# A rank projection in two products instead of three, an earlier sixth product in Strassen rows, and finer task steps, in a two-layer backbone on one core

## The chip, the cores and the metric

The kernel runs on one core of a Trainium2 chip. The metric is the time of one launch on the device, in microseconds (us). Engines are called as in the profile: PE (TensorE: matrix products), DVE (VectorE), ACT (ScalarE), POOL (GpSimd) and SP (SyncE, which issues most DMAs).

## The reference, cut to what matters

One inference step of a two-layer diffusion backbone over 128 context and 512 latent tokens, model width 2048. Each layer is a modulated RMS norm, one wide in-projection, two mixers side by side, a SiLU gate, an output projection and a gated residual. Layer 0 mixes by windowed attention and by gated linear attention (GLA), layer 1 by neighbourhood attention and a gated MLP.

The part whose products the change rewrites is the low-rank gate of the GLA. The in-projection yields, besides q, k, v and the gates, 2 x 16 columns `rb`; they go through small weights to the gate of each channel:

```python
GLA_RANK = 16
EVEN_SPLITS = (H_A * HEAD_DIM, KV_A * HEAD_DIM, KV_A * HEAD_DIM,
               H_B * DK_B, H_B * DK_B, H_B * DV_B, 2 * GLA_RANK, MIX_W)
...
    r = rb.reshape(B, T, 2, GLA_RANK)
    logit = jnp.einsum('btdr,drk->btdk', r, wg) + bg
    g = (jax.nn.log_sigmoid(logit.astype(jnp.float32)) / GLA_NORMALIZER).reshape(B, T, 2, H_B, DK_B)
```

All is float32.

## The kernel before, in words

**Products.** Every float32 operand is split in two parts of a shorter format, a high part `h` (ACT writes it, a copy with rounding) and a low part `l` (POOL or DVE: the value less the high part). In the trace these are `acth`/`actl` for activations, `whi`/`wlo` for weights, `eh`/`el` and `fh`/`fl` for sums. A product is three matmuls into the same bank of accumulators: hi by h, hi by l, lo by h (`mm_k`, L862). The activations lie feature by feature: 16 columns k of 128 features by 640 tokens, and each matmul takes one k and one half of the tokens (320 columns, 322 where two columns of shift ride along).

**Weights.** `wpump` (from about L790) loads weight tiles ahead of their use, copies the high part with ACT and subtracts with POOL or DVE. For the rank projection `w_rb` (L2513, `add(d["w_rb"], 96, ...)`) the 32 columns are written three times, as three blocks of a stationary operand of 96 columns; rows 0 to 95 of the result then hold r three times, which `gla_rank` (L2010) splits into high and low for the next product with `wgs` (three blocks likewise, `gla_wg`, L2000).

**Layer-0 in-projection.** `chunk` and `units` (L887) run over chunks of 128 output columns, four k at a time for each half, and call `tick` on the way. There are three banks for these sums; a bank is emptied by DVE (`lin`: `arena<-bank,rstd`, then `bc<-bank`) once its last matmul is done. `tick(n)` (L543) lets waiting tasks make up to n steps: the steps of the GLA scan, the attention heads, the rewriting. What is left of DVE's time goes to the `low` task, the reductions of the adaLN weights (`ada`), which are a DVE instruction of 512 elements each. A model of the engines' times (`Pace`, L41) decides when a task may step; it runs while the program is built, so the order of each engine's instructions is fixed. `calm(lag)` (L575) lets a task go on only when the modelled queues of DVE and ACT are at most `lag` us ahead.

**Output projections and layer 1.** They use Strassen's scheme over pairs of output chunks, in rows: `steps` (L658) gives the order of the products of a pair (A11, A12, S1, S2, S4, S3, A22), `spair` (L1000) issues them, `strassen_jobs` (L671) the sums of weights that they need. The last pair of each of three rows (`ends`) reloads, behind its S3, the half columns of `acth`/`actl` that were folded to sums (`unfold`, L1258, DMAs `acth<-bh_dram`), which the next plain pair needs.

**Handover** (L1127). Between two layers the result, column by column, is scaled and split into `acth`/`actl` (`rewrite`, an order of k given by hand), and for the pairs of columns the half sums `eh`/`el` are formed (`fold`, with `split`, L1175). Three handovers are in the program: y0 (at about 800 us), x1 (about 1050) and y1. `rewrite` and `fold` share DVE and ACT, and both wait by `calm(3.0)`.

Of the kernel before, what the change touches and what calls it, by code (L numbers as in the profile page):

```python
# [245 lines left out]
class Trunk:  # L246
# [412 lines left out]
    def steps(self, c1, c2):  # L659

        names = lambda *x: [(c1, f) for f in x]
        if self.count[c1] == ALL:
            return names("A11", "A12", "S1", "S2", "S4", *(("S3", "A22") if c1 in self.ends else ("A22", "S3")))
        return [*names("A11"), (c1, PLAIN, 0), *names("A12", "S1", "S2", "S4"), (c2, PLAIN, 0), *names("S3", "A22")]
# [7 lines left out]
    def strassen_jobs(self, c1, c2, last, unit):  # L672
# [25 lines left out]
        add = lambda o, a, b, op: ("add", lambda: (piece(o), piece(a), piece(b)), op, 4 in (o, a, b))  # L698
# [9 lines left out]
        if ns == ALL:  # L708
            after = {("A12", 8): [add1], ("S1", 5): [add2], ("S2", 5): [add3], ("S4", 5): [add4]}
            assert all(t in [k + m for k, m in self.blocks_of(ns, f)] for f, t in after)  # L710
# [43 lines left out]
    def wpump(self, force=False):  # L754
# [63 lines left out]
        if m < M:  # L818
            raw = raw[:, :, None, :].to_broadcast([128, n, M // m, m])
            hi, lo = (x.rearrange("p a (b c) -> p a b c", c=m) for x in hl)  # L820
        nc.scalar.activation(hi, raw, AF.Copy)
# [40 lines left out]
    def mm_k(self, c, k, outs, first=0, last=KT - 1, r=0):  # L862
# [4 lines left out]
        todo = []  # L867
        for p, half in outs:
            cs = self.cols(half, shift)
            h, l = self.ah[:, k, cs], self.al[:, k, cs]  # L870
            todo += [(0, p, hi, h, k == first, False), (1, p, hi, l, False, False), (2, p, lo, h, False, k == last)]
# [11 lines left out]
    def units(self, c, k0, evac):  # L883

        p, done = [], self.ahead.pop(c, None)
        for k in range(k0, KT, 4):
            for half in range(2):  # L887
                if k == k0:
                    p.append(done if half and done is not None else self.pj())
                for j in range(k, k + 4):  # L890
                    if p[half] is not done:
                        self.mm_k(c, j, [(p[half], half)], k0)
                    if j % 2:
                        self.tick(2)
# [90 lines left out]
    def spair(self, c1, c2):  # L985
# [70 lines left out]
        end = self.steps(c1, c2)[-1]  # L1056
        for key in self.steps(c1, c2):
            f = key[1]
            if len(key) == 3 and key[0] == c1:
# [10 lines left out]
            elif f == "S1":  # L1070
                plus(full(xa), x)
                ev1(xa, None)
                self.drop(xa)
                v = take()
                self.need("T124")
                product(v, full, f, tt(0))
            elif f == "S2":
                product(t, full, f, tt(1))
                x = copy(half(t))
                plus(x, half(v))  # L1080
            elif f == "S4":
# [4 lines left out]
                self.drop(xb)  # L1086
            elif f == "S3":
                self.need("T3")
                product(t, half, f, J(x2))
                if c1 in self.ends:  # L1090
                    self.spawn(self.unfold(ns), first=True)
# [2037 lines left out]
```

## Time and profile before

| | |
|---|---|
| median of 3 runs | 2050.56 us (2047.29 to 2052.04) |
| the profiled execution's own time | 2051.18 us |
| its span in the trace | 2049.4 us |
| mean granted PE clock | 0.996 |
| PE instructions | 14255 |

The page gives shares of the span; the table of stretches cuts the span at given times and gives each engine's busy time there; the timeline gives single instructions in the form "start, duration, engine, line, operation, out<-in, shape", and in square brackets how long the engine stood idle before and which result ended that. L219 is the line of a helper through which all engine instructions go, L449 that of all matmuls, L454 of transpositions on PE, L492 of SP's DMAs. Durations of matmuls overlap: the pace is read from start to start.

### The profile page before, as it was taken

The numbers are of one execution on the slowest core, as the hardware profiler recorded it, in microseconds if no ns is written. First come the engines' busy times: TensorE is split into PE (matmuls) and PEld (weight loads), VectorE is DVE, ScalarE is ACT, GpSimd is POOL, SyncE is SP. The second block draws the span as 40 slices with busy tenths as digits, with TensorE's granted clock in tenths as the row PEclk, the third lists the DMA queues.
The fourth block names the chain that finished last, engine by engine and source line by source line (L and its number), as shares of the span: only waits on it lengthen the run. The fifth ranks groups of instructions, "written<-read, shape, count | busy, mean of one in ns | idle before, by whom it ended". The sixth has DMA issues, their size and how long they took to land.

```text
span 2049.4 us, 40331 instructions
## 1 busy us (share of the span) xinstructions
PE 2012.4 (98%) x14255; PEld 1976.9 (96%) x14255; DVE 1356.0 (66%) x3175; ACT 1098.7 (54%) x2430; POOL 1362.9 (67%) x1096
## 2 busy tenths in 40 slices
PE   8999999999999999999999999999999999999997
PEld 6899999999999999999989999999999999999997
DVE  4656677476557666898577787656665677568444
ACT  5445555445564766544465444565565654455443
POOL 5555465446556555798755777766766688878884
PEclk9999999999999999999999999999999999999999
DMA  9965433336456455577534434444344354265437
GB/s 376 400 208 163 143 112 102 121 119 185 156 184 215 148 179 179 174 242 230 186 107 138 134 126 132 133 132 130 120 147 126 120 174 154 91 216 194 144 98 277
DMA packets 234316, 344.13 MB, mean 168 GB/s; under 512 B 22049, under 2 KB 139649, under 8 KB 234113
## 3 DMA queue, kind: packets, MB, share of 16 engines
q1 hardware_dynamic: 232912, 340.38, 50.7%
q8 instruction: 112, 1.84, 0.4%
q10 hardware_dynamic: 1200, 1.17, 0.2%
q14 instruction: 92, 0.75, 0.1%
HBM read 304.99 MB, written 33.85 MB: 165 GB/s over the span
## 4 chain that ended last, share of the span: by engine, by line
PE 87%; DMA 6%; DVE 3%; ACT 2%; issue 1%; POOL 1%; SPq 0%; DVEq 0%; POOLq 0%; ACTq 0%
PE bank L449 84%; PE bank L454 2%; DMA more<-ada 1%; DMA Y<-ada 1%; DVE bank L219 1%; DVE arena L219 1%; DVE Y L219 1%; DMA arena<-yT_dram 1%; PE bank L1605 0%; DMA Y<-xT 0%; ACT acth L219 0%; DMA wraw<-w_even 0%; DMA wraw<-w_out 0%; DVE rs L219 0%; DMA rawx<-ada_g 0%
## 5 line engine op out<-in xcount | busy, mean ns | idle before, releaser
L449 PE MATMUL bank<-acth,whi 128*128 128x320 f32 (+3 forms) x3072 | 941.0, 318 | 6.8 <-DVE bc L219 2.8
L449 PE MATMUL bank<-actl,whi 128*128 128x320 f32 (+3 forms) x3072 | 917.0, 310 | 1.3 <-POOL actl L219 1.3
L449 PE MATMUL bank<-acth,wlo 128*128 128x320 f32 (+3 forms) x3072 | 915.6, 310 | 0.0
L219 POOL TENSOR_TENSOR wlo<-wraw,whi 128x512 fp32r<-128x512 f32 (+2 forms) x415 | 531.3, 1290 | 395.3 <-ACT whi L219 360.4
L449 PEld LDWEIGHTS bank<-acth,whi 128*128 128x128 f32 (+1 forms) x3072 | 569.1, 188 | 14.7 <-issue 4.1
L449 PEld LDWEIGHTS bank<-actl,whi 128*128 128x128 f32 (+1 forms) x3072 | 569.6, 188 | 3.5 <-POOL actl L219 1.5
L449 PEld LDWEIGHTS bank<-acth,wlo 128*128 128x128 f32 (+1 forms) x3072 | 568.6, 188 | 0.8 <-POOL wlo L219 0.6
L219 POOL TENSOR_TENSOR wlo<-rs,whi 128x384 fp32r<-128x384 f32 (+2 forms) x370 | 457.7, 1262 | 111.4 <-ACT whi L219 78.5
L219 ACT ACTIVATE whi<-wraw 128x512 fp32r<-128x512 f32 (+2 forms) x425 | 245.8, 586 | 164.1 <-PE bank L449 85.2
L219 ACT ACTIVATE whi<-rs 128x384 fp32r<-128x384 f32 (+2 forms) x370 | 191.9, 536 | 100.8 <-PE bank L449 45.7
L449 PE MATMUL bank<-eh,whi 128*128 128x322 f32 (+1 forms) x666 | 209.5, 314 | 0.0
L449 PE MATMUL bank<-el,whi 128*128 128x322 f32 (+1 forms) x666 | 206.4, 310 | 0.0
L449 PE MATMUL bank<-eh,wlo 128*128 128x322 f32 (+1 forms) x666 | 206.3, 310 | 0.0
L219 POOL TENSOR_TENSOR prod<-adas,mixrow 128x512 f32<-128x512 f32 x93 | 121.1, 1313 | 50.6 <-ACT prod L219 32.4
L219 DVE TENSOR_TENSOR bank<-bank,sums 128x320 f32<-128x320 f32 (+1 forms) x148 | 70.1, 495 | 95.8 <-ACT sums L219 47.9
L449 PEld LDWEIGHTS bank<-eh,whi 128*128 128x128 f32 x666 | 125.4, 188 | 0.0
L449 PEld LDWEIGHTS bank<-eh,wlo 128*128 128x128 f32 x666 | 125.4, 188 | 0.0
L449 PEld LDWEIGHTS bank<-el,whi 128*128 128x128 f32 x666 | 125.3, 188 | 0.0
L219 DVE CUSTOM_DVE_ANT_0 adas<-adas,bank,part 128x512 bf16<-128x512 f32 x146 | 108.6, 744 | 22.6 <-DMA adas<-ada 15.7
L219 POOL TENSOR_TENSOR wlo<-adas,whi 128x512 fp32r<-128x512 f32 x62 | 80.2, 1300 | 44.0 <-ACT whi L219 43.5
L219 ACT ACTIVATE sums<-bank 128x320 f32<-128x320 f32 (+1 forms) x111 | 48.2, 434 | 103.6 <-PE bank L449 97.4
L219 DVE CUSTOM_DVE_ANT_0 adas<-adas,bank 128x512 bf16<-128x512 f32 x107 | 73.2, 684 | 13.6 <-DMA adas<-ada 5.2
(287 smaller groups left out, 3057.6 us busy)
## 6 DMA issues: line engine op xcount, KB each, us to landing
wraw<-w_even SPq DMA_DIRECT2D x176, 256.0 KB, 3.3
rs<-w_odd SPq DMA_DIRECT2D x150, 256.0 KB, 3.3
adas<-ada SPq DMA_DIRECT2D x128, 256.0 KB, 3.8
adas<-ada_g SPq DMA_DIRECT2D x64, 256.0 KB, 3.8
rs<-w_out SPq DMA_DIRECT2D x60, 256.0 KB, 3.7
adas<-w_odd SPq DMA_DIRECT2D x50, 256.0 KB, 3.8
Y<-ada SPq DMA_DIRECT2D x24, 512.0 KB, 7.7
more<-ada SPq DMA_DIRECT2D x24, 512.0 KB, 7.8
```

The costliest lines, as they stand in the source:

```text
L219: return f(*args, **kw)
L449: self.nc.tensor.matmul(out, lhsT, rhs, start=start, stop=stop, **kw)
L454: self.nc.tensor.transpose(out, in_, self.ident[:k, :k])
```

## The change

Four edits.

1. The rank projection takes 128 columns, the 32 weight columns four times: blocks low, high, high, high. One product of 128 columns (all blocks by h) and one of 32 columns (a high block by l, into rows 0 to 31) take the place of three products of 96 columns, for each k and half: 64 matmuls instead of 96. The next product contracts 128 rows instead of 96.
2. In a row's last pair of 25 pairs' rows the order is A11, A12, S2, S1, S3, S4, A22 (before: A11, A12, S1, S2, S4, S3, A22); in the last pair of the row of output projection 0 S3 comes ahead of the second plain product. The last weight sum is made in two halves.
3. The half sums of a handover wait by `calm(1.5)` instead of 3.0 until the last column is rewritten.
4. In `units` tasks may make one step after an even k and two after an odd one, instead of two after an odd one.

The diff's core:

```diff
@@ steps
         if self.count[c1] == ALL:
-            return names("A11", "A12", "S1", "S2", "S4", *(("S3", "A22") if c1 in self.ends else ("A22", "S3")))
-        return [*names("A11"), (c1, PLAIN, 0), *names("A12", "S1", "S2", "S4"), (c2, PLAIN, 0), *names("S3", "A22")]
+            return names("A11", "A12", *(("S2", "S1", "S3", "S4", "A22") if c1 in self.ends else ("S1", "S2", "S4", "A22", "S3")))
+        last = [*names("S3"), (c2, PLAIN, 0)] if c1 in self.ends else [(c2, PLAIN, 0), *names("S3")]
+        return [*names("A11"), (c1, PLAIN, 0), *names("A12", "S1", "S2", "S4"), *last, *names("A22")]
@@ strassen_jobs
             after = {("A12", 8): [add1], ("S1", 5): [add2], ("S2", 5): [add3], ("S4", 5): [add4]}
+            if c1 in self.ends:
+                after = {("A11", 8): [add1], ("A12", 4): [add2], ("S2", 5): [add3], ("S1", 5): [add(4, 3, 2, ALU.subtract, (0, 4))], ("S1", 8): [add(4, 3, 2, ALU.subtract, (4, 8))]}
@@ wpump
         if m < M:
-            raw = raw[:, :, None, :].to_broadcast([128, n, M // m, m])
-            hi, lo = (x.rearrange("p a (b c) -> p a b c", c=m) for x in hl)
-        nc.scalar.activation(hi, raw, AF.Copy)
+            hi, lo = hi.rearrange("p a (b c) -> p a b c", c=m), hi[:, :, 0:m]
+            nc.scalar.activation(hi, raw[:, :, None, :].to_broadcast([128, n, M // m, m]), AF.Copy)
+            hi, hl = lo, [hl[0], hl[0]]
+        else:
+            nc.scalar.activation(hi, raw, AF.Copy)
@@ mm_k
+            if m < M:
+                n = h.shape[1]
+                self.mm(p[:M, :n], hi, h, start=k == first, stop=k == last, skip_group_check=True)
+                self.mm(p[:m, :n], hi[:, m : 2 * m], l, start=False, stop=k == last, skip_group_check=True)
+                continue
@@ units
-                    if j % 2:
-                        self.tick(2)
+                    self.tick(1 + j % 2)
@@ handover, split
-            yield from self.calm(self.calms[1])
+            yield from self.calm(self.calms[1] if f"{ready}:{order[-1]}" in self.flags else 1.5)
@@ gla_dir, gla_rank, in-projection, weights
-            self.mm(ps[:, :HT], L["wgs"][0:96, 128 * dr : 128 * dr + 128], L["r"][0:96, c])
+            self.mm(ps[:, :HT], L["wgs"][:, 128 * dr : 128 * dr + 128], L["r"][:, c])
...
-        nc.scalar.activation(r[0:96, :], x[0:96, :], AF.Copy)
-        nc.vector.tensor_tensor(r[64:96, :], x[64:96, :], r[64:96, :].bitcast(F32), ALU.subtract)
+        nc.scalar.activation(r, x, AF.Copy)
+        nc.vector.tensor_tensor(r[96:128, :], x[96:128, :], r[96:128, :].bitcast(F32), ALU.subtract)
...
-        add(d["w_rb"], 96, True, None, lazy("vt", rows=96, then=lambda x: self.spawn(self.gla_rank(x))))
+        add(d["w_rb"], 128, True, None, lazy("vt", then=lambda x: self.spawn(self.gla_rank(x))))
```

Edits 3 and 4 change the order of the engines' instructions through the model. Two places show how.

On DVE, in the layer-0 in-projection at 338 to 346 us of the trace before: `Y` and the first operand `arena` are the GLA's scan (the two `SCALAR_TENSOR_TENSOR` rows are its scans, listed as TENSOR_TENSOR_SCAN in the trace), and `arena<-bank_69,rstd` with `bc<-bank_69` empties a projection bank. Before:

```order
L219 TENSOR_SCALAR Y<-bank_70,small 128x320
L219 TENSOR_TENSOR Y<-Y,arena_1683 128x640
L219 SCALAR_TENSOR_TENSOR arena_1683<-arena_1683,Y 128x640
L219 TENSOR_TENSOR Y<-Y 128x640
L219 SCALAR_TENSOR_TENSOR Y<-arena_1683,Y 128x640
L219 TENSOR_TENSOR arena_1683<-bank_69,rstd 128x320
L219 TENSOR_SCALAR bc_2820<-bank_69 128x2
```

And of the change:

```order
L219 TENSOR_SCALAR Y<-bank_70,small 128x320
L219 TENSOR_TENSOR Y<-Y,arena_1665 128x640
L219 SCALAR_TENSOR_TENSOR arena_1665<-arena_1665,Y 128x640
L219 TENSOR_TENSOR arena_1665<-bank_69,rstd 128x320
L219 TENSOR_SCALAR bc_2801<-bank_69 128x2
L219 TENSOR_TENSOR Y<-Y 128x640
L219 SCALAR_TENSOR_TENSOR Y<-arena_1665,Y 128x640
```

The emptying of the bank has moved ahead of a product and a scan.

On ACT, in the handover x1 at 1048 to 1060 us of the trace before: `rs`, `adas` and `arena` are columns of x1 (`<-...,A` scales one, `acth<-` writes its high part; the one from `adas` is k = 1, the one from `arena` k = 3), `eh<-bank` is the high part of a half sum, `whi<-wraw` a split of weights. Before:

```order
L219 ACTIVATE acth<-rs_8045 128x640
L219 ACTIVATE whi<-wraw 128x512
L219 ACTIVATE eh_8043<-bank_69 128x320
L219 ACTIVATE adas<-adas,A_97 128x128
L219 ACTIVATE adas<-adas,A_97 128x512
L219 ACTIVATE acth<-adas 128x640
L219 ACTIVATE whi<-wraw 128x512
L219 ACTIVATE eh_8043<-bank_73 128x320
L219 ACTIVATE arena_8050<-arena_8050,A_97 128x512
L219 ACTIVATE acth<-arena_8050 128x640
```

And of the change:

```order
L219 ACTIVATE acth<-rs_8067 128x640
L219 ACTIVATE whi<-wraw 128x512
L219 ACTIVATE adas<-adas,A_97 128x128
L219 ACTIVATE adas<-adas,A_97 128x512
L219 ACTIVATE acth<-adas 128x640
L219 ACTIVATE eh_8065<-bank_73 128x320
L219 ACTIVATE whi<-wraw 128x512
L219 ACTIVATE rstd<-bank_72,eps 128x320
L219 ACTIVATE rstd<-rstd 128x320
L219 ACTIVATE arena_8072<-arena_8072,A_97 128x128
L219 ACTIVATE arena_8072<-arena_8072,A_97 128x512
L219 ACTIVATE acth<-arena_8072 128x640
```

The `eh` that stood between the weight split and column 1 is gone from there, and one half sum fewer stands ahead of column 3.

More of the change, by code (lines that the diff above doesn't have):

```diff
@@ L696, in load @@
             )
-        add = lambda o, a, b, op: ("add", lambda: (piece(o), piece(a), piece(b)), op, 4 in (o, a, b))
+        add = lambda o, a, b, op, r=(0, ns): ("add", lambda: (piece(o, *r), piece(a, *r), piece(b, *r)), op, 4 in (o, a, b))
         if last is None:
@@ L866, in mm_k @@
         hi, lo = (x[:, i, :] for x in self.wget((c, u, r)))
-        todo = []
+        todo, m = [], w.shape[2]
         for p, half in outs:
@@ L1056, in spair @@
         end = self.steps(c1, c2)[-1]
+        done = set()
         for key in self.steps(c1, c2):
             f = key[1]
+            done.add(key)
             if len(key) == 3 and key[0] == c1:
@@ L1069, in spair @@
                 product(xa, full, f, M(x1))
[L1070 to L1080, printed above, removed]
+            elif f in ("S1", "S2"):
+                if xa:
+                    plus(full(xa), x)
+                    ev1(xa, None)
+                    self.drop(xa)
+                    xa = None
+                    self.need("T124")
+                if f == "S1":
+                    v = take()
+                    product(v, full, f, tt(0))
+                else:
+                    product(t, full, f, tt(1))
+                    x = copy(half(t))
+                if {(c1, "S1"), (c1, "S2")} <= done:
+                    plus(x, half(v))
             elif f == "S4":
@@ L1086, in spair @@
                 self.drop(xb)
+                if (c1, "S3") in done:
+                    x = copy(full(t))
+                    self.drop(t)
             elif f == "S3":
@@ L1091, in spair @@
                     self.spawn(self.unfold(ns), first=True)
+                if xb is None:
+                    continue
                 x = copy(full(t))
@@ L2002, in gla_wg @@
         nc, wg, ws = self.nc, self.L["wg"], self.L["wgs"]
-        self.dma(wg[0:96, :], self.d["gla_wgp"][:, h])
-        yield from self.until(wg[0:96, :])
-        nc.scalar.activation(ws[0:96, :], wg[0:96, :], AF.Copy)
-        nc.vector.tensor_tensor(ws[32:64, :], wg[32:64, :], ws[32:64, :].bitcast(F32), ALU.subtract)
+        self.dma(wg, self.d["gla_wgp"][:, h])
+        yield from self.until(wg)
+        nc.scalar.activation(ws, wg, AF.Copy)
+        nc.vector.tensor_tensor(ws[64:96, :], wg[64:96, :], ws[64:96, :].bitcast(F32), ALU.subtract)
         self.flags.add(f"wg{h}")
@@ L3082, in _layout @@
         wg[16 * i : 16 * i + 16, :, i] = a["gla_wg"][0, i].reshape(16, 4, 128)
-    o["gla_wgp"] = np.concatenate([wg.reshape(32, 4, 256)] * 3, 0)
+    o["gla_wgp"] = np.concatenate([wg.reshape(32, 4, 256)] * 4, 0)
     o["gla_bgT"] = feat(a["gla_bg"][0])
```

## The prediction

> **What bounds the kernel now.** I read the page first: busy shares, then the chain.
>
> ```profile
> span 2049.4 us, 40331 instructions
> PE 2012.4 (98%) x14255; PEld 1976.9 (96%) x14255; DVE 1356.0 (66%) x3175; ACT 1098.7 (54%) x2430; POOL 1362.9 (67%) x1096
> PE 87%; DMA 6%; DVE 3%; ACT 2%; issue 1%; POOL 1%; SPq 0%; DVEq 0%; POOLq 0%; ACTq 0%
> ```
>
> TensorE (PE) is busy for 98% of the span and the chain is PE for 87%. So the time changes in two ways only: fewer matmuls, or less waiting of PE. Where PE waits, the table of stretches shows (us of the stretch, then PE busy and its instructions; the last three columns are granted clock, DMA share, GB/s).
>
> ```profile
> 118.00:300.00 182.00, 182.00 (x1251) 180.62 (x1250) 121.91 (x245) 98.84 (x202) 99.33 (x77) 1.00 0.47 148
> 300.00:360.00 60.00, 57.97 (x389) 56.93 (x388) 41.92 (x71) 33.55 (x67) 33.30 (x24) 0.97 0.29 94
> 360.00:500.00 140.00, 140.00 (x971) 138.21 (x970) 88.62 (x169) 67.03 (x137) 70.45 (x50) 1.00 0.43 138
> 500.00:540.00 40.00, 38.02 (x259) 37.37 (x258) 23.30 (x70) 20.60 (x49) 25.88 (x20) 1.00 0.64 187
> 790.00:860.00 70.00, 68.85 (x465) 68.23 (x464) 49.68 (x99) 34.91 (x73) 46.89 (x33) 1.00 0.58 187
> 1005.00:1080.00 75.00, 71.22 (x463) 69.47 (x462) 48.01 (x96) 48.66 (x102) 40.63 (x30) 0.98 0.44 152
> 1165.00:1640.00 475.00, 475.00 (x3316) 473.54 (x3315) 323.04 (x933) 261.23 (x615) 337.52 (x282) 1.00 0.41 130
> 1700.00:2000.00 300.00, 300.00 (x2039) 299.76 (x2038) 186.52 (x298) 150.25 (x319) 252.06 (x194) 1.00 0.46 147
> 2038.00:2050.00 12.00, 0.00 (x0) 0.00 (x0) 5.76 (x14) 0.54 (x2) 4.57 (x7) 0.56 0.84 287
> ```
>
> PE idles 2.0 us in 300–360, 2.0 in 500–540, 1.2 in 790–860 and 3.8 in 1005–1080, where the rewriting of x1 stands; the two long stretches of layer 1 have none. The last 12 us, without PE, are the final norm, which the change leaves alone. In 300–360 and 1005–1080 the granted clock is below 1 as well. The table asked again for two short pieces there:
>
> ```profile
> 346.40:349.80 3.40, 3.40 (x16) 3.36 (x15) 2.66 (x4) 1.90 (x6) 0.00 (x0) 0.50 0.00 0
> 1059.80:1063.20 3.40, 3.40 (x13) 3.40 (x14) 2.21 (x2) 3.34 (x8) 2.68 (x2) 0.50 0.23 76
> ```
>
> Each is 3.4 us at half the clock, so each costs 3.4 x 0.5 = 1.7 us beyond the wait that precedes it. [...]
>
> **The rank chunk.** The timeline of PE at its start and its end:
>
> ```profile
> 139.42 0.31 PE L449 MATMUL bank<-acth,whi 128*96 128x320 f32 x1
> ...
> 145.42 0.31 PE L449 MATMUL bank<-acth,wlo 128*96 128x320 f32 x1
> 145.56 0.27 PE L454 MATMUL bank<-ident,old 128*32 128x128 f32 x1
> 145.59 0.39 PE L449 MATMUL bank<-acth,whi 128*96 128x320 f32 x1
> 145.82 0.30 PE L449 MATMUL bank<-actl,whi 128*96 128x320 f32 x1
> ...
> 153.63 0.31 PE L449 MATMUL bank<-acth,whi 128*128 128x322 f32 x1
> ```
>
> From 139.42 to 153.63 are 14.21 us for 96 matmuls (16 k, two halves, three products) and one small transposition. 139.42 to 145.42 is 6.00 us for 41 of them, 0.146 each; durations of 0.31 overlap. A matmul's price is its number of moving columns, not the 96 or 128 weight columns (the wider ones at 153.63 follow at the same pace in the trace). So 32 matmuls fewer are 32 x 0.147 = **-4.7 us**, on PE's path, where nothing else ran beside them that must now be waited for: PE idles nowhere between 118 and 300 us, so what supplies it has room.
>
> What can eat this is the new shape: each 128-column product is followed by a 32-column one. Rows of products of 32 columns exist for the conditioning vectors:
>
> ```profile
> 99.66 0.30 PE L449 MATMUL bank<-acth,wlo 128*128 128x320 f32 x1
> 99.90 0.64 PE L1605 MATMUL bank<-Y,cond 128*32 128x128 f32 x16
> ...
> 102.33 0.41 PE L449 MATMUL bank<-acth,whi 128*128 128x320 f32 x1
> 102.58 0.31 PE L449 MATMUL bank<-actl,whi 128*128 128x320 f32 x1
> ```
>
> Into them 0.24 us pass instead of 0.147, out of them 0.25: 0.20 us for a change there and back. But at 145.56, in this very chunk, a 32-column step between two of 96 takes nothing extra (0.14 us into it, and 0.26 from it to the second matmul after, which is one matmul of 0.147 and 0.11 for the step itself). Bounds: 0 to 32 x 0.20 = 6.4 us. I take 0, the row nearest in place, and keep the other as a rival. ACT's copy of the weights grows from 384 to 512 elements and the subtraction shrinks from 384 to 128, both off the path; the gate product contracts 128 rows instead of 96 at the same pace.
>
> **Finer ticks in the whole layer-0 in-projection.** Three task steps instead of two per two k; the order of DVE, ACT and POOL is reshuffled there, so each wait has to be looked at again. The worst one:
>
> ```profile
> 340.20 1.85 DVE L219 TENSOR_TENSOR Y<-Y 128x640 f32<-128x640 f32 x1
> 342.08 2.46 DVE L219 TENSOR_TENSOR_SCAN Y<-arena,Y 128x640 f32<-128x640 f32 x1
> 344.46 0.46 DVE L219 TENSOR_TENSOR arena<-bank,rstd 128x320 f32<-128x320 f32 x1
> 344.85 0.14 DVE L219 TENSOR_SCALAR bc<-bank 128x2 f32<-128x2 f32 x1
> ```
>
> ```profile
> 345.04 0.41 PE L449 MATMUL bank<-acth,whi 128*128 128x320 f32 x1 [2.03 <-DVE bc L219]
> ```
>
> A projection bank is emptied behind a 1.85 and a 2.46 us step of the gated attention's scan; PE waits 2.03 us for it. In the new order (DVE rows shown with the change) the emptying stands ahead of both, 4.3 us sooner, less one reduction of about 0.7 that is new ahead of it. 3.6 is more than 2.03, so the wait goes and with it the half clock: **-3.7 us**. The other end is 0, if the emptying still finds its bank late. Next late is the following bank, behind the same scan's rest, which waited for nothing before.
>
> The price: reductions of the adaLN weights come earlier too. Counted in the order, between PE's 3000th and 4000th matmul DVE has 93 of them instead of 66.
>
> ```profile
> L219 DVE CUSTOM_DVE_ANT_0 adas<-adas,bank,part 128x512 bf16<-128x512 f32 x146 | 108.6, 744 | 22.6 <-DMA adas<-ada 15.7 <-ACT bank L219 4.1
> 465.00:610.00 145.00, 143.02 (x953) 137.70 (x952) 85.98 (x263) 82.54 (x200) 81.83 (x63) 1.00 0.56 177
> ```
>
> 27 x 0.744 = 20 us more on DVE in a stretch of some 145 us in which it is busy for 86: 106 of 145. It fits, but a bank that is emptied after an extra reduction comes 0.7 us later, and two or three in a row make a wait. Bounds: -1 (a short wait elsewhere goes) to +6; I take one wait like that at 345 without the half clock, **+2 us**. The first attention head adds its own:
>
> ```profile
> 531.71 0.49 PE L449 MATMUL bank<-arena 128*128 128x128 f32 x2 [1.31 <-DVE arena L219]
> ```
>
> In the new order this product stands 6 matmuls closer to the rotary step that it waits for: 6 x 0.147 = **+0.9 us** (0, if the finer steps start the rotary step sooner, to 2.6 with a half clock).
>
> **Strassen rows and the handover x1.** S3 one product earlier in the rows' last pairs lets the reloading of the half columns start about 24 matmuls (24 x 0.147 = 3.5 us) sooner. No wait of PE at a row's end goes back to that reloading, so it buys nothing itself; what follows it on SP's queue (`w_out` weights) moves up by 13 matmuls, 1.9 us. The last weight sum is now made in two halves before S3; ends of rows in 1165–2000 had no PE wait, and I cost the new place at nothing, with POOL's and ACT's splitting as the cover (1.3 + 0.6 us a row if it is gone). The gain is in the chain at x1:
>
> ```profile
> 1039.91 0.78 PE L449 MATMUL bank<-acth,whi 128*128 128x322 f32 x2 [1.25 <-DVE Y L219]
> ...
> 1057.94 0.57 PE L449 MATMUL bank<-acth,whi 128*128 128x322 f32 x2 [0.94 <-ACT acth L219]
> 1059.79 0.90 PE L449 MATMUL bank<-actl,whi 128*128 128x322 f32 x2 [1.28 <-POOL actl L219]
> ```
>
> ```profile
> 1052.65 0.61 ACT L219 ACTIVATE whi<-wraw 128x512 fp32r<-128x512 f32 x1
> 1055.78 0.44 ACT L219 ACTIVATE eh<-bank 128x320 fp32r<-128x320 f32 x1 [2.52 <-DVE bank L219]
> 1056.12 1.00 ACT L219 ACTIVATE adas<-adas,A 128x128 f32<-128x128 f32 x2
> 1057.15 0.74 ACT L219 ACTIVATE acth<-adas 128x640 fp32r<-128x640 f32 x1
> ```
>
> ACT stood 2.52 us before an `eh` of a half sum, with the scaling and the rewriting of column 1 queued behind it, and PE waited for both parts of that column. Now the half sums yield until the last column is rewritten: the new ACT order (shown with the change) has no `eh` between the weight split and that column. Counted in the order, its first part stands 39 matmuls ahead of its use instead of 22: 17 x 0.147 = 2.5 us, against waits of 0.94 + 1.28 = 2.2. So that wait and its half clock go (2.2 + 1.7 = 3.9), and of the 1.25 at 1039.91 about half, since ACT's weights come 1.9 us sooner but DVE's order there stays. Next late is column 3, whose second part stands 19 matmuls ahead (15 before) while PE now arrives without the 3.9 us that covered it: I give back 0.7. **-3.9 - 0.6 + 0.7 = -3.8 us**; ends -5.2 and -1.
>
> **Sum**: -4.7 - 3.7 + 2.0 + 0.9 - 3.8 = -9.3 us. The profiled execution took 2051.2 us (span 2049.4 and 1.8 around it), 0.6 above the median; 2051.2 - 9.3 = 2041.9, so **2042 us**.
>
> **Rivals.** Drain (0.25): the 32-column products behave like the conditioning rows, 6.4 us on the rank chunk, 2042 + 6 = 2048. For it: a product, not a transposition, as in the new code. Against: the row at 145.56. [...]
>
> Waits move on (0.20): only the matmuls go; the 345 wait reappears a bank later, column 3 takes over from column 1. -4.7 + 0.9 - 1 = about -5, 2046.5.
>
> DVE is overfilled (0.09), the slower side: reductions ahead of bank emptyings cost PE a wait of 2.0 plus half a clock window of 1.7, 3.7 each. A bank has 24 matmuls, 3.5 us, until it is needed again; the point is where DVE's queue ahead of an emptying exceeds that. The forecast without its 2 us allowance is -11.3; four such waits give 2051.2 - 11.3 + 14.8 = 2054.7, five 2058. For it: 20 us of moved DVE work, and 345 shows the mechanism. Against: one wait of that size between 118 and 500 us, with DVE busy for 63 to 70% of the stretches.
>
> **How the numbers follow.** The forecast has 0.46. A measurement of this kernel tells about 0.2%, 4 us, from no change: faster is below 2046.5, slower above 2054.7. Forecast: 0.43 faster, 0.03 same. Drain: 0.08 and 0.16, 0.01 slower. Waits move on: 0.10 and 0.10. Overfilled: 0.03 same, 0.06 slower. Together 0.61, 0.32, 0.07. The low end takes the good ends of the terms (-4.7 - 3.7 - 5.2 - 1 = -14.6, 2036.6), the high end drain with one further wait of 3.7 (2048 + 3.7): 2036 to 2052.
>
> **What the changed profile would show.** Right: 64 matmuls from the rank chunk's start to its end, 9.4 us; no wait by `bc` near 340 and no clock of 0.50 there; no wait by `acth` or `actl` near 1050, or one below 1 us. Wrong: 0.2 us steps inside the rank chunk (drain); new DVE waits of 2 us between 360 and 700 (overfilled); waits by `actl` a column later. What would overturn the forecast as a whole is new waiting between 118 and 700 us above 6 us.

## The result and the profile after

The changed kernel takes 2042.53 us (median of 8 runs, 2037.76 to 2046.67), the kernel before 2047.05 us beside it (8 runs, 2045.09 to 2052.04). The ratio is 0.9973, with an interval of 0.9961 to 0.9986: 5.5 us faster (0.0027 x 2047), between 2.9 and 8.0. The forecast was 2042 us, from the profiled execution's 2051.18 less 9.3. The profiled execution of the changed kernel took 2042.48 us, so between the two profiles are 8.7 us; the kernel before's own profile lies near the top of its runs, which makes the difference of the profiles larger than that of the medians. Where the 8.7 us went can be followed from stage to stage; it is not the sum that was forecast, though it comes to nearly the same.

The page of the changed kernel: span, PE's busy time, the shares of the chain.

```profile
span 2040.7 us, 40294 instructions
PE 2007.1 (98%) x14223; PEld 1971.3 (97%) x14223; DVE 1357.9 (67%) x3172; ACT 1104.5 (54%) x2436; POOL 1366.8 (67%) x1096
PE 89%; DMA 5%; DVE 3%; ACT 2%; issue 1%; POOL 1%; SPq 0%; DVEq 0%; ACTq 0%; POOLq 0%
```

PE has the 32 matmuls less that edit 1 takes away (14255 before) and is still busy for 98% of the span. The table of stretches, for the stretches that the prediction showed:

```profile
118.00:300.00 182.00, 178.90 (x1222) 174.62 (x1221) 127.09 (x248) 103.32 (x205) 99.11 (x78) 1.00 0.48 148
300.00:360.00 60.00, 60.00 (x411) 59.08 (x411) 46.91 (x81) 33.03 (x64) 30.96 (x22) 1.00 0.35 113
360.00:500.00 140.00, 140.00 (x968) 138.07 (x968) 89.54 (x181) 68.34 (x139) 68.98 (x50) 1.00 0.46 147
500.00:540.00 40.00, 36.92 (x235) 36.31 (x234) 25.16 (x77) 21.64 (x52) 25.37 (x20) 0.91 0.58 185
790.00:860.00 70.00, 70.00 (x478) 70.00 (x477) 50.45 (x102) 36.89 (x75) 49.16 (x35) 1.00 0.61 200
1005.00:1080.00 75.00, 75.00 (x508) 74.68 (x507) 48.72 (x105) 53.57 (x115) 42.94 (x31) 1.00 0.55 185
```

300–360, 790–860 and 1005–1080 have lost every idle time (2.0, 1.2 and 3.8 us before) and run at full clock. 118–300, which had none, now has 3.1 us, and 500–540 has 3.1 instead of 2.0 and a clock of 0.91. So waits went at three places and came at two. The table of PE's waits (total us, times, longest) names the new ones:

```profile
PE bank L454 <- ACT arena L219: 3.7, 4, 1.9
PE bank L449 <- ACT adas L219: 3.2, 3, 2.2
PE bank L454 <- DVE old L219: 1.7, 1, 1.7
```

The waits by `arena` (L454, transpositions of an attention head) stand at 502–504 us (3.1 of the 3.7) and the one by `old` at 145 us; before, PE waited at neither place. The `adas` row belongs to the lead stage, in front of the change.

**The rank chunk.** PE's timeline, first and second part of the chunk:

```profile
138.44 0.31 PE L449 MATMUL bank<-acth,whi 128*128 128x320 f32 x1
138.58 0.31 PE L449 MATMUL bank<-actl,whi 128*32 128x320 f32 x1
138.73 0.31 PE L449 MATMUL bank<-acth,whi 128*128 128x320 f32 x1
...
142.98 0.31 PE L449 MATMUL bank<-actl,whi 128*32 128x320 f32 x1
144.96 0.28 PE L454 MATMUL bank<-ident,old 128*32 128x128 f32 x1 [1.67 <-DVE old L219]
145.23 0.41 PE L449 MATMUL bank<-acth,whi 128*128 128x322 f32 x1
...
150.06 0.31 PE L449 MATMUL bank<-acth,whi 128*128 128x322 f32 x1
```

The products of 128 and 32 columns follow each other at 0.147 us, so the new shape costs nothing. From the chunk's start to the next chunk's are 11.62 us instead of 14.21. That is 2.6 less, not 4.7, since the transposition in the middle (the conditioning step) now waits: 1.98 us lie between it and the product before it, 1.83 more than the pace. DVE, at the same place:

```profile
143.01 0.75 DVE L219 CUSTOM_DVE_ANT_0 adas<-raw,bank,old 128x512 bf16<-128x512 f32 x1
...
143.87 0.84 DVE L219 TENSOR_TENSOR old<-old,rawx 128x8 f32<-128x8 f32 x4
144.62 0.28 DVE L219 TENSOR_TENSOR old<-old,small 128x8 f32<-128x8 f32 x2
```

And DVE's row in the kernel before, where PE reached that transposition at 145.56:

```profile
144.43 0.29 DVE L219 TENSOR_TENSOR old<-old,small 128x8 f32<-128x8 f32 x2
```

The step needs the reductions of the adaLN shifts, which DVE ends at 144.72 us (before) and 144.90 (after). The chunk's first part is the work that PE is given meanwhile. Before, PE came to the step 0.84 us after DVE had ended (145.56 less 144.72). The two chunks start 0.98 us apart, so the times are counted from the chunk's start: PE is ready for the step after 4.69 us instead of 6.14, which is 1.45 earlier, and DVE ends after 6.46 us instead of 5.30, which is 1.16 later. 1.45 and 1.16 less the 0.84 in hand are 1.77, the wait but for 0.06 from DVE's end to PE's start. In the order that the model builds, DVE now has 50 of the 64 reductions that it shares with POOL, 48 before, at 0.75 us each.

**The new waits near 500 us.** PE's, DVE's and ACT's timelines there:

```profile
501.73 0.33 PE L454 MATMUL bank<-ident,arena 128*128 128x128 f32 x1 [1.18 <-ACT arena L219]
...
503.96 1.12 PE L454 MATMUL bank<-ident,arena 128*128 128x128 f32 x4 [1.90 <-ACT arena L219]
```

```profile
500.02 0.75 DVE L219 CUSTOM_DVE_ANT_0 adas<-adas,bank,partg 128x512 bf16<-128x512 f32 x1 [3.67 <-ACT bank L219]
...
500.69 0.49 DVE L219 TENSOR_TENSOR arena<-bank,rstd 128x320 f32<-128x320 f32 x1
...
501.99 0.75 DVE L219 CUSTOM_DVE_ANT_0 adas<-adas,bank,partg 128x512 bf16<-128x512 f32 x1 [0.75 <-DMA adas<-ada_g]
...
502.66 0.49 DVE L219 TENSOR_TENSOR arena<-bank,rstd 128x320 f32<-128x320 f32 x1
```

```profile
499.28 0.60 ACT L219 ACTIVATE bank<-adas 128x512 f32<-128x512 f32 x1 [2.82 <-DMA adas<-crow_s]
...
501.28 0.40 ACT L219 ACTIVATE arena<-arena,bc 128x128 f32<-128x128 f32 x1 [0.85 <-DVE bc L219]
```

Start with the cause of the first wait: ACT stands 2.82 us before the copy of a condition row that a DMA has not yet brought. DVE stands 3.67 us before a reduction that needs this copy, and the emptying of a finished bank (500.69) is queued behind that reduction. ACT's scaling of `arena` waits for the emptying, and PE for the scaling. The second wait has a late operand of its own: the other half's emptying (502.66) is queued behind the next reduction, which stood 0.75 us for its weights (`ada_g`, 501.99). Six other profiles have both waits; there the first is 0.6 to 1.7 us and the second always 1.9. The clock falls to half between the two, for 6.8 us:

```profile
502.59:509.42 6.83, 5.46 (x22) 5.47 (x23) 5.00 (x15) 4.36 (x11) 3.68 (x4) 0.50 0.64 199
```

With it the place costs 6.0 us by the start times of the matmuls from 500 to 510 us, of which 1.18 + 1.90 are the waits.

**The handover x1.** ACT's timeline, where the order shown with the change stands:

```profile
1046.45 0.61 ACT L219 ACTIVATE whi<-wraw 128x512 fp32r<-128x512 f32 x1
1046.97 1.00 ACT L219 ACTIVATE adas<-adas,A 128x128 f32<-128x128 f32 x2
1048.00 0.74 ACT L219 ACTIVATE acth<-adas 128x640 fp32r<-128x640 f32 x1
1048.65 0.42 ACT L219 ACTIVATE eh<-bank 128x320 fp32r<-128x320 f32 x1
```

Column 1 follows the weight split at once, and no matmul waits between 1005 and 1080. Some new idle time is in the row of output projection 1 instead, by the low part of a weight sum:

```profile
1857.25 0.41 PE L449 MATMUL bank<-eh,wlo 128*128 128x320 f32 x1 [0.23 <-POOL wlo L219]
```

This, and two steps like it up to 1862, lose 1.3 us against the pace.

**The sum by stages**, from the start times of the same matmuls in the two profiles (after less before): up to the rank chunk -1.0; rank chunk -2.6; to 360 us -1.0 (the wait and half clock at 345 -3.8, three new waits at 254, 262 and 274 +1.8, the rest +1.0); 360–500 +0.2; 500–790 +4.2 (new waits and half clock at 502 to 510 +6.0, the waits at 531 and 534 -2.3, one at 609 +0.6, the rest -0.1); 790–860 -1.8; x1 -6.7; 1080–1165 -1.6; 1800–1880 +1.4; elsewhere +0.2. Together -8.7.

### The profile page after: what moved, and what is told of

Read it like the earlier page. It is cut to its first block, busy times and chain, and to the rows that moved or that the text cites. A ratio compares the mean times of both kernels' runs of the same rounds, so it can differ in the third digit from the quotient of the medians.

```text
span 2040.7 us, 40294 instructions
## 1 busy us (share of the span) xinstructions
PE 2007.1 (98%) x14223; PEld 1971.3 (97%) x14223; DVE 1357.9 (67%) x3172; ACT 1104.5 (54%) x2436; POOL 1366.8 (67%) x1096
## 3 DMA queue, kind: packets, MB, share of 16 engines
q8 instruction: 111, 1.82, 0.4%
## 4 chain that ended last, share of the span: by engine, by line
PE 89%; DMA 5%; DVE 3%; ACT 2%; issue 1%; POOL 1%; SPq 0%; DVEq 0%; ACTq 0%; POOLq 0%
PE bank L449 86%; PE bank L454 2%; DMA wraw<-w_even 1%; DVE adas L219 1%; POOL wlo L219 1%; DVE arena L219 1%; DVE Y L219 1%; DMA adas<-ada 1%; DMA adas<-ada_g 1%; DMA more<-ada 0%; DMA Y<-ada 0%; ACT arena L219 0%; DMA raw<-ada_s 0%; PE bank L1625 0%; DMA crow_s<-adas 0%
## 5 line engine op out<-in xcount | busy, mean ns | idle before, releaser
L449 PE MATMUL bank<-acth,whi 128*128 128x320 f32 (+2 forms) x3072 | 940.5, 318 | 1.4 <-DVE YB L219 0.7
L449 PE MATMUL bank<-acth,wlo 128*128 128x322 f32 (+3 forms) x3040 | 905.4, 310 | 0.0
L449 PEld LDWEIGHTS bank<-acth,whi 128*128 128x128 f32 x3072 | 569.8, 188 | 9.1 <-issue 2.6
L449 PEld LDWEIGHTS bank<-acth,wlo 128*128 128x128 f32 x3040 | 563.4, 188 | 0.3 <-POOL wlo L219 0.2
L219 POOL TENSOR_TENSOR wlo<-rs,whi 128x384 fp32r<-128x384 f32 (+2 forms) x370 | 463.0, 1275 | 108.6 <-ACT whi L219 78.5
L219 ACT ACTIVATE prod<-prod 128x512 f32<-128x512 f32 x109 | 67.8, 623 | 27.8 <-POOL prod L219 27.7
```

The costliest lines, as they stand in the source:

```text
L219: return f(*args, **kw)
L449: self.nc.tensor.matmul(out, lhsT, rhs, start=start, stop=stop, **kw)
```

## The experiments

The theory after the result had three parts. The rank chunk's first part is cover for DVE's shift reductions, and its saving is not cashed. The finer steps (edit 4) pay at 345 us and lose at 500. Yielding half sums (edit 3) carry x1. The rivals are named in each expectation. Ratios are to the kernel before, timed on the same chip, with 95% intervals; 0.001 is 2.0 us.

**Edit 1 alone.** The kernel before with the hunks of edit 1 (`wpump`, `mm_k`, `gla_dir`, `gla_rank`, `w_rb`) and no others. In this kernel and the next, columns 8 to 11 of layer 0's mixed output (part of the GLA's) are made from other operands than the reference's; every instruction is issued, so the work is the same.

> Edit 1 alone on the kernel before. Theory (the terms add up by place): the rank chunk loses 32 x 0.147 = 4.7 us and nothing else changes on PE, so 4 to 5 us faster than before (ratio about 0.9977); the waits at 345, 531, 1040 and 1058 us stay where they were, 4.7 us earlier. Rival (the saving is taken back by a wait): the conditioning step of the adaLN task inside the rank chunk, for which PE waited 1.7 us in the changed kernel, is due to the shorter chunk itself and appears here too; then 3 us or less.

Measured: 2045.55 us, 0.9992 (0.9981 to 1.0002): not 4 to 5 us faster but 1.6, and not clear of none. The step of this kernel:

```profile
145.03 0.28 PE L454 MATMUL bank<-ident,old 128*32 128x128 f32 x1 [1.66 <-DVE old L219]
```

The rival is right: the wait comes with edit 1 alone, so it is not a matter of edit 4's order, and DVE has 50 reductions here too. The clock falls to half right behind it (0.55 granted in 145.60–149.00), and the second part of the chunk, from the step to the next chunk, takes 6.63 us instead of the changed kernel's 5.10. From the chunk's start to the next chunk's are 13.1 us instead of 14.2. So 1.1 us is all that the chunk gains where the half clock follows.

**Edit 4 undone.**

```diff
-                    self.tick(1 + j % 2)
+                    if j % 2:
+                        self.tick(2)
```

> The changed kernel with edit 4 undone (two steps after every odd k, as before). Theory: finer ticks gave the wait at 345 away (3.7 us with its half clock) and brought new waits at 145, 254 to 275, 502 to 504 and 609 us with a half clock of their own, together about 8 us; without them the kernel is about 4 us faster than the changed one (ratio to before about 0.995), the wait at 345 is back and the one at 502 is gone. Rival: finer ticks are a gain and the wait at 502 comes from elsewhere (a slow DMA of that one execution); then without them it is 2 to 4 us slower than the changed kernel (ratio to before about 0.9985).

Measured: 2041.24 us, 0.9973 (0.9961 to 0.9984), the same as the changed kernel. PE's timeline shows the old wait again:

```profile
342.94 0.41 PE L449 MATMUL bank<-acth,whi 128*128 128x320 f32 x1 [1.51 <-DVE bc L219]
```

No half clock follows it here (300–360 at 1.00). The waits at 502 and 504 are gone, and 500–540 has no idle time; a wait of 1.75 us by `wlo` stands at 844, with a half clock (790–860 at 0.98). So each theory's place was right and neither's sum: beside the other edits, edit 4 loses in other places about what it wins at 345.

**Edit 3 undone, and edit 2 undone**, two kernels.

```diff
-            yield from self.calm(self.calms[1] if f"{ready}:{order[-1]}" in self.flags else 1.5)
+            yield from self.calm(self.calms[1])
```

> The changed kernel with edit 3 undone (half sums wait by calm(3.0) throughout). Counted in the order of instructions, column 1 of x1 is then written 30 matmuls ahead of its use (22 before the change, 39 after it), column 3 27 (19 and 23). Theory: the yielding of half sums carries the gain at x1; without it about half of the wait at column 1 is back, 1 to 2 us, and the half clock with it if the idle time reaches 2 us: 1 to 4 us slower than the changed kernel. Rival: the earlier S3 carries it; then no wait over 0.5 us at x1 and the same time as the changed kernel.

The other takes back the hunks of `steps`, `strassen_jobs` and `spair`.

> The changed kernel with edit 2 undone (order of the last pairs as before). Column 1 of x1 is then 28 matmuls ahead of its use, column 3 20. Theory: the earlier S3 only moves a queue; without it column 1 still keeps most of its lead, a wait of up to 1 us returns at x1 and at 1040, and the waits of 1.3 us at 1857 (weights of a row's last pair) go: within 1.5 us of the changed kernel. Rival: the earlier S3 carries the gain at x1, then 1040 and 1058 are both back, 4 to 6 us slower than the changed kernel.

Measured: without edit 3 2043.68 us, 0.9989 (0.9975 to 1.0002); without edit 2 2043.44 us, 0.9987 (0.9975 to 0.9998). By the ratios each is about 3 us slower than the changed kernel, but the intervals overlap with the changed kernel's, so the places say more than the times. (The profile without edit 3 is of an execution 7 us above that kernel's median.) Without edit 3, x1 waits again, by `actl`:

```profile
1057.64 0.56 PE L449 MATMUL bank<-actl,whi 128*128 128x322 f32 x2 [0.88 <-POOL actl L219]
...
1060.40 0.56 PE L449 MATMUL bank<-actl,whi 128*128 128x322 f32 x2 [0.72 <-POOL actl L219]
```

1005–1080 is 3.4 us shorter than before instead of 6.7, and the waits by ACT's `adas` at 1134 and 1152 (0.45 and 1.32) are back. Without edit 2 only one wait is left at x1 (0.40 at 1037), so x1 is edit 3's, but for that last wait, which edit 2 takes away. Near 1857 the loss is not one edit's: without edit 2 it is all there (0.4 + 0.3 + 0.9 in three steps), and without edit 3 one step of 0.5 is left, as with edit 4 alone (further down), while the two steps ahead of it go. So these two come with edit 3.

**Which part of the rank chunk counts.** The second product issued twice for one half of the tokens:

```diff
+                if half == 0:
+                    self.mm(p[:m, :n], hi[:, m : 2 * m], l, start=False, stop=False, skip_group_check=True)
                 self.mm(p[:m, :n], hi[:, m : 2 * m], l, start=False, stop=k == last, skip_group_check=True)
```

> The changed kernel with the second product of the rank chunk issued twice in its first half: 16 matmuls more, 16 x 0.147 = 2.35 us of PE work (what it changes in the result: the part high by low is counted twice in that half). Theory: the first half's saving was never cashed, because the conditioning step between the halves, with its wait of 1.7 us for the adaLN reductions of the shift on DVE, ends when those end; then the wait shrinks to about 0 and the kernel is at most 0.7 us slower than the changed one (0.5 us: 2.35 less 1.83). Rival: the reductions are pushed on with the chunk's end and the wait stays: 2.4 us slower than the changed kernel, wait still near 1.7.

> The same 16 extra matmuls in the second half (the part high by low counted twice there). Theory: nothing bounds that half but PE, so 2.35 us slower than the changed kernel, in the profile between the conditioning step and the next chunk; the wait of 1.7 us ahead of it stays. Rival: a wait behind the chunk swallows it; then no change by the start of the scan at 250 us.

The program issues half 1 (320 columns) ahead of the waiting transposition and half 0 (322) behind it, so each label and its expectation belong to the other place in time. With `half == 1`, PE's timeline at the step:

```profile
143.28 0.46 PE L449 MATMUL bank<-actl,whi 128*32 128x320 f32 x2
143.66 0.28 PE L454 MATMUL bank<-ident,old 128*32 128x128 f32 x1
143.92 0.41 PE L449 MATMUL bank<-acth,whi 128*128 128x322 f32 x1
```

The wait is gone: 16 matmuls more (2.35 us) ahead of the step lengthen the chunk by 0.56, from 11.62 to 12.18, and the time doesn't show it: 2041.17 us, 0.9967 (0.9955 to 0.9980). PE and DVE now come to the step together, and DVE's end has moved too, to 7.02 us behind the chunk's start (49 reductions on DVE). With `half == 0` the wait stays (1.69) and the second part takes 8.98 us, at half clock for a while (118–200 at 0.98), 2.35 more than in edit 1 alone, where the half clock follows as well: 2044.49 us, 0.9987 (0.9977 to 0.9996; this interval overlaps with the changed kernel's). This is what the theory asks: of 2.35 us in the first part 0.56 count, in the second all.

**More of the shift reductions on POOL** (24 of 64 instead of 14), to end DVE's part sooner: `self.mixed = 1.5` around the loop over the shifts.

> The changed kernel with POOL allowed 1.5 us of queue for products of the shift's reductions: 24 of 64 go to POOL instead of 14, DVE keeps 40 instead of 50. Theory: DVE's reductions end before the first half of the rank chunk does, so the wait of 1.7 us in the middle of the chunk goes: 1.8 us faster than the changed kernel. Rival: POOL's products push its weight splits back in the lead stage and PE waits for weights there instead: no gain or slower by up to 2 us.

Measured: 2043.43 us, 0.9980 (0.9971 to 0.9988).

```profile
146.41 0.28 PE L454 MATMUL bank<-ident,old 128*32 128x128 f32 x1 [2.20 <-DVE old L219]
```

The wait grew. The theory is wrong, and of the rival the time comes true but not the mechanism: PE's waits for weights (`wlo`) are 1.3 us in all, as in the changed kernel when run again. DVE has fewer reductions, but at its end it stands 0.51 us for weights of the shifts (`ada_s`) and 0.56 for ACT's copy of a product that POOL made; it ends 6.99 us behind the chunk's start instead of 6.46. DVE's share alone doesn't set the end of the shifts.

**Another chunk as cover.** The first `k` chunk of the GLA (three products) goes ahead of the rank chunk:

```diff
-        add(d["w_rb"], 128, True, None, lazy("vt", then=lambda x: self.spawn(self.gla_rank(x))))
         for h in range(4):
...
             add(wE[16 + h], 128, True, None, lazy("k", pre=p))
+            if h == 0:
+                add(d["w_rb"], 128, True, None, lazy("vt", then=lambda x: self.spawn(self.gla_rank(x))))
```

> The changed kernel with the rank chunk second and the k chunk of the first GLA head first in the layer-0 in-projection. The part of the first chunk that is issued ahead of the conditioning step is then 48 matmuls (7.0 us) instead of 32 (4.7 us). Theory: the wait of 1.7 us in the middle of the chunk is what kept edit 1 from its 4.7 us; it goes (2.35 us more cover against 1.83), with the half clock that followed it in some executions: 2 to 3 us faster than the changed kernel. The condition row of group g0 now stands 57 matmuls behind its DMA instead of 33, so the waits at 502 shrink too. Rival: the reductions move on with the longer part, as the order of DVE is fixed by the model, and the wait stays: same time as the changed kernel.

Measured: 2039.64 us, 0.9966 (0.9954 to 0.9979). The wait at the step is gone, DVE has 48 reductions of the shifts again, and the rank chunk, now without the step in its middle, takes 9.40 us: 64 matmuls at 0.147, all that edit 1 can save. New waits are at 195.7 (1.64, by `bc`) and 258 (1.08), those at 531 and 534 are back (1.03 at 529 and 0.66 at 532), and one is at 503:

```profile
503.03 0.66 PE L454 MATMUL bank<-ident,arena 128*128 128x128 f32 x4 [2.34 <-ACT arena L219]
```

```profile
500.27 0.75 DVE L219 CUSTOM_DVE_ANT_0 adas<-adas,bank,partg 128x512 bf16<-128x512 f32 x1 [1.54 <-DMA adas<-ada_g]
...
501.73 0.49 DVE L219 TENSOR_TENSOR arena<-bank,rstd 128x320 f32<-128x320 f32 x1
```

Here the reduction at the head of DVE's queue waits for its weights (`ada_g`), not for the row, and the emptying is again queued behind it. No half clock follows this wait of 2.34 us (500–540 at 1.00).

**The condition row copied later.** The copy of that one row waits for 2.5 us more of modelled time, so that other steps go ahead of it:

```diff
             if len(job) == 2:
+                if job[1] == 3 and todo[i + 2][2][0] == "g0":
+                    yield 2.5
```

> The changed kernel with 2.5 us more of modelled time ahead of the copy of one condition row (group g0, fourth quarter), so that ACT's copy and the reduction behind it stand some 21 to 33 matmuls later in the order. Theory: the waits at 502 and 504 us (1.2 + 1.9, with a half clock of 1.7) come from that row alone: its DMA lands late, DVE stands 3.7 us at a reduction that needs it, and a bank's emptying is queued behind; they go, and the kernel is 3 to 5 us faster than the changed one. Rival: DVE is simply overfilled there; the wait then moves to the next bank and the time stays within 1 us.

Measured: 2040.33 us, 0.9957 (0.9943 to 0.9970). The waits at 502 and 504 and their half clock are gone (6.0 us by start times; 490–510 at 1.00): the later copy moves that quarter's reductions behind the emptyings of both halves. In the profiled execution another comes at 823:

```profile
823.38 0.94 PE L449 MATMUL bank<-acth,whi 128*128 128x320 f32 x2 [3.31 <-ACT eh L219]
```

It goes back to a DMA that ACT stood 3.65 us for (`arena<-yT_dram`). With its half clock (6.8 us long; 0.50 granted in 823.40–827.80) it loses 6.1 us there, so this profile is only 0.6 us shorter than the changed kernel's, while the ratios differ by 0.0016, 3.3 us, with intervals that overlap; whether that late DMA is in every execution isn't shown.

**Edit 4 alone**, on the kernel before.

> Edit 4 alone on the kernel before. Theory: the finer ticks take away the wait at 345 with its half clock (3.7 us) and bring waits at 254 to 275 (1.8 us); in its order the condition row of group g0 stands 57 matmuls behind its DMA, not 33, so there is no wait at 502: 1 to 3 us faster than before (ratio about 0.999), with x1's waits at 1040 and 1058 as before. Rival: the waits at 502 are a matter of the finer ticks alone, not of that row; they are there too and the time is 1 to 3 us above that of the kernel before.

Measured: 2052.07 us, 1.0023 (1.0012 to 1.0034): 4.7 us slower, so the theory's time is missed, and the rival has the direction alone. Its profile, of an execution 3 us below that median (2049.09), has the wait at 345 gone, those at 255 to 276 (1.7 together) come, 0.48 at 503, 1.79 at 530, and x1 as before. Its span is 2.1 us shorter than that of the kernel before (2047.3 and 2049.4), whose profile lies above its own median. So the profile doesn't show the 4.7, and what makes them stays open.

**The changed kernel again.**

> The changed kernel itself, beside the two others on the same chip. Theory: as measured first, 0.996 to 0.999 of the kernel before; in some of its executions a half clock follows the wait inside the rank chunk (1.5 us), in others not. Rival: none; it is the mark for the other two.

Measured: 2041.73 us, 0.9973 (0.9962 to 0.9984). The step waits for 1.67 us as in the first profile, and this time the clock falls behind it:

```profile
145.13:148.54 3.41, 3.41 (x14) 2.76 (x14) 0.00 (x0) 0.63 (x2) 1.28 (x1) 0.50 0.43 110
```

**Both cures together**: the other chunk as cover, and the row later by 5.0.

> The kernel of the swap with the condition row of group g0, fourth quarter, held back by 5 us of modelled time, so that DVE's first reduction of that quarter stands behind the emptying of both banks at 498 to 502 us (in the swap's kernel three of them stood ahead of the first one). Theory: what stopped DVE there was a reduction whose data were still on their way, not the number of reductions; the wait of 2.5 us at 503 goes, with its half clock: 2 to 4 us faster than the swap's kernel, ratio to the kernel before about 0.995. Rival: later reductions cost as much at the handover y0, as a DMA wait of 3.5 us did at 823 in the kernel with the late row alone; then no faster than the swap's kernel.

Measured: 2033.89 us (2032.12 to 2036.54), 0.9938 (0.9924 to 0.9951): 12.7 us faster than before (10.0 to 15.6), and apart from the changed kernel's 0.9973 on the same chip (0.9962 to 0.9984). That is 5.7 us faster than the exchange alone, where 2 to 4 were expected; 4.3 us between the two profiles are won from 500 to 540 us, where the waits at 529 and 532 go too. The table of stretches and DVE's timeline at the place of the old wait:

```profile
118.00:200.00 82.00, 80.20 (x541) 78.08 (x541) 57.36 (x123) 45.13 (x93) 44.44 (x37) 1.00 0.51 164
300.00:360.00 60.00, 60.00 (x417) 59.33 (x416) 45.34 (x77) 35.95 (x71) 30.00 (x21) 1.00 0.37 122
500.00:540.00 40.00, 40.00 (x279) 39.81 (x279) 29.07 (x90) 22.82 (x54) 23.68 (x20) 1.00 0.60 193
```

```profile
494.30 0.49 DVE L219 TENSOR_TENSOR arena<-bank,rstd 128x320 f32<-128x320 f32 x1 [1.95 <-PE bank L449]
...
496.07 0.49 DVE L219 TENSOR_TENSOR arena<-bank,rstd 128x320 f32<-128x320 f32 x1 [1.21 <-PE bank L449]
496.48 0.74 DVE L219 CUSTOM_DVE_ANT_0 adas<-adas,bank,partg 128x512 bf16<-128x512 f32 x1
```

The emptyings stand ahead of the reductions, and now DVE waits for PE rather than PE for DVE. Against the changed kernel's profile, 5.9 of the 8.6 us are won between 400 and 600 us. What is left behind the lead stage is a wait of 1.64 at 193 that came with the exchange of the chunks, 1.06 at 256 and 0.78 at 1852.

## Why the prediction was right, and where its steps were not

**What bounds the kernel.** Right: all that changed the profile's time was a matmul less, a wait of PE or the half clock behind one, and the stages' sums show them.

**The rank chunk, -4.7.** The count (32 matmuls at 0.147) and the choice of the bound 0 for the new shape were right: the alternating products keep the pace (0.147 us), and drain, the first rival, is refuted. The trace of the kernel before has the price by moving columns: 0.117 us at 256 (from 2033.66), 0.147 at 320, 0.174 at 384 (from 2014.06), and 0.147 with 96 weight columns as with 128. The step that failed is "PE idles nowhere between 118 and 300 us, so what supplies it has room". No idle time doesn't say how much room there is: the row of DVE at 144.43 gives it, 0.84 us. Nor does the supplier stand still while PE's work shrinks: the order built for the shorter chunk leaves DVE two reductions more, and it ends 1.16 us later behind the chunk's start. The mechanism was right for the second part of the chunk; the first part's saving became a wait of 1.83. Measured -2.6, or about -1.1 where the half clock follows; edit 1 alone and the two kernels with a longer half show it, and with another chunk as cover the rank chunk takes the 9.4 us that the prediction gave it.

**345 us, -3.7.** Right: wait and half clock are gone, and 3.8 us are won; without edit 4 the wait is back (1.51). The half clock in it, 1.7 of the 3.7, is not in every profile: it follows the wait in the kernel before, but not without edit 4 (300–360 at 1.00).

**The price of the moved reductions, +2.0, and the first head, +0.9.** The sign was right and the place half right. Three waits by `bc`, `Y` and `arena` at 254 to 274 cost 1.8. But 531, which was to grow by 0.9, is gone in the changed kernel (-2.3), and 6.0 came at 502 to 510. The prediction's picture of an overfilled DVE (so many reductions ahead of an emptying, at 0.7 us each) isn't what happened: DVE had time to stand still for 3.67 us. One reduction whose row was still on its way held up an emptying, and the next, whose weights were late, the other. The later copy of that one row moves both behind the emptyings and takes the waits away, and the exchanged chunks alone make such a wait out of late weights. Waits and half clock at 500 were mis-sized as a term: +4.2 for the stage, where +0.9 stood.

**x1, -3.8.** The mechanism was right (undoing edit 3 brings the waits back) and the size too small: measured -6.7. The residue that was given back for column 3 (0.7) isn't there, and the wait at 1039.91 goes wholly, where half was taken. Two further gains were not seen at all: 828 and 857 us (-1.8), in the handover y0, and ACT's `adas` transpositions at 1136 and 1153 (-1.6). Both gains are in the profile of edit 4 alone as well (-1.7 and -1.8).

**Strassen rows, nothing.** Nearly: the row ends in layer 1 have no wait but the one at 1857 to 1862, 1.3 us, which was costed at nothing, with POOL's splitting as the cover. It is there without edit 2 too, so the rows' new order isn't its cause; two of its three steps come with edit 3, and the third is there with edit 4 alone.

**The sum.** -9.3 was forecast and -8.7 lies between the profiles, with errors of both signs: +2.1 at the rank chunk, +4.3 for the moved reductions and the first head (154 to 790 us without 345: 2.8 + 0.2 + 4.2 = 7.2, where 2.9 stood) and +1.4 at 1857, against -2.9 at x1, -3.4 at the places not foreseen and -1.0 ahead of the rank chunk. The ratio gives less than the profiles (-5.5), since the kernel before was profiled in an execution about 4 us above its median of 8 runs. The prediction took it for 0.6 above, on three runs. So the time came out right in part because a too large gain was taken from a too high start: that is luck. By its own sign the forecast as a whole was overturned, too: new waiting between 118 and 700 us was to stay below 6 us, and it is 6.5 us of idle time at 145, 254 to 274, 502 to 504 and 609, without the half clock. The gains at x1 and at the places not foreseen paid for it.

"Waits move on" was the nearest of the rivals: waits did move, but to the step in the rank chunk and to the head at 500, not to the next bank or from column 1 to column 3.

## What to carry to other kernels

Matmuls taken out of a stretch are worth their time only if nothing else was timed to end with that stretch: look for the next wait by reading, on the engine that supplies it, when its last instruction ends, and not whether PE idles now; and where a model builds the order, read that end again in the new order, counted from the start of the stretch. An instruction whose data may be late belongs behind those for which PE waits, on an engine like DVE here, which stood 3.67 us before one reduction with the emptying of a finished bank queued behind it: one copy moved, and the reductions with it, took 6.0 us of waits and half clock away. A forecast that starts from one profile inherits that profile's place among its runs, 4 us above the median here: compare the start with many runs, not with three.

## What the runs showed of the hardware

The half clock is not a fixed price of a wait. The same wait at the same step (1.82 to 1.85 us beyond the pace) was followed by 3.4 us at half clock in five of the profiled kernels (edit 1 alone, edit 4 undone, edit 2 undone and half 0 longer, each with 118–200 at 0.98, and the changed kernel again, 0.50 in 145.13–148.54: the chunk's second part at 6.63, with the longer half 8.98), and by full clock in three (the changed kernel's first profile, edit 3 undone, the late row, each with 118–200 at 1.00: 5.1). The changed kernel is in both lists, so the program doesn't decide it; between its two profiles it is 1.5 us.

The traces give the times of the changes. In the kernel before the clock fell at 346.42 and 1059.80 us and came back at 349.83 and 1063.21, 3.41 us later each time; the two falls lie 713.38 us apart, 209 times 3.4133. PE had idled for 2.03 and 2.21 of the 3.41 us ahead of them:

```profile
343.01:346.42 3.41, 1.38 (x10) 1.38 (x10) 3.41 (x6) 1.40 (x4) 0.18 (x1) 1.00 0.34 121
1056.39:1059.80 3.41, 1.20 (x5) 0.42 (x4) 1.95 (x6) 3.35 (x7) 1.83 (x2) 1.00 0.17 59
```

In the changed kernel's first profile the fall at 502.59 came after 1.71 us of idle time in 3.41. The clock stayed low for twice 3.41 us, with 1.37 us of idle time in the first of them and none in the second:

```profile
499.18:502.59 3.41, 1.70 (x11) 1.25 (x9) 1.83 (x5) 1.55 (x3) 1.93 (x2) 1.00 0.76 277
502.59:506.00 3.41, 2.04 (x9) 2.05 (x10) 3.19 (x10) 2.82 (x7) 2.04 (x3) 0.50 0.62 180
506.00:509.42 3.42, 3.42 (x15) 3.42 (x15) 1.81 (x6) 1.54 (x5) 1.64 (x2) 0.50 0.65 217
```

The stretches around the conditioning step, first of the changed kernel again, up to its fall at 145.13, then of its first profile, counted back by 3.413 us from the fall at 502.59:

```profile
141.72:145.13 3.41, 1.74 (x12) 1.11 (x11) 2.25 (x11) 1.25 (x5) 1.25 (x3) 1.00 0.04 14
```

```profile
140.78:144.19 3.41, 2.51 (x18) 1.90 (x16) 3.16 (x10) 1.45 (x4) 2.59 (x3) 1.00 0.25 77
144.19:147.61 3.42, 2.65 (x17) 2.16 (x18) 0.77 (x6) 1.14 (x3) 0.61 (x3) 1.00 0.12 37
```

In the one the whole wait lies in one stretch, 1.67 us of 3.41 idle, and half clock follows; in the other two stretches share it, 0.90 and 0.77, and none follows. The length of a wait alone doesn't decide it either: full clock followed the 2.34 us at 503 in the exchanged kernel (500–540 at 1.00), half clock the 1.67 us here. What does decide it isn't shown.

Products of 128 x 128 and 128 x 32 in turn keep the pace at 320 columns: 32 starts in a row, 0.147 us apart, where the conditioning rows of the kernel before took 0.24 us into the 32-column products and 0.25 out of them.
